# A two-layer hybrid encoder on one core: the opening's third transfer is made to wait for the first, and eighteen opening products stand for twenty-two

## The chip, the cores and the metric

The kernel runs on one core of a Trainium2 chip. The metric is the device time in microseconds (us). The kernel before was run three times; a run with the hardware profiler was taken beside these. The core has five engines that work side by side: TensorE (PE; its weight loads are listed as PEld), VectorE (DVE), ScalarE (ACT), GpSimd (POOL) and SyncE (SP). In this kernel SP computes nothing, it issues nearly all transfers from the chip's memory, one after another in a fixed order.

## The reference, cut to what matters

Two layers work on 256 frames of width 2048. In each, one wide input projection feeds three groups of heads, and one output projection joins them:

```python
h = x @ w_in
a_q, a_k, a_v, a_z, b_q, b_k, b_v, b_z, b_lr, m_q, m_z = jnp.split(h, cuts, axis=-1)
y_a = chunk_band_attention(heads_a(a_q), heads_a(a_k), heads_a(a_v), rel_table)
o_b = gla_chunk_recurrence(heads_k(b_q), heads_k(b_k), b_v, heads_k(log_g))
mkv = mem @ w_mem_kv
mk, mv = jnp.split(mkv, 2, axis=-1)
y_m = memory_attention(heads_m(m_q), heads_m(mk), heads_m(mv))
y = jnp.concatenate([y_a * silu(a_z), y_b * silu(b_z), y_m * silu(m_z)], axis=-1)
return layer_norm(DEEPNORM_ALPHA * x + y @ w_out, ln_g, ln_b)
```

The kernel does not begin with `x` but with `mem`, the 256 fixed memory tokens: the projection `mem @ w_mem_kv` is the first work of a layer. Its second half `mv` comes from the weights `G_MV`, its first half `mk` from `G_MK`. These activations and weights are what the opening transfers bring.

## The kernel before, in words

**Two-part products.** Every float32 matrix that TensorE multiplies is split into a high part, a rounded copy that ScalarE makes (a CAST), and a low part, the float32 rest that VectorE makes with one subtraction (a TENSOR_TENSOR). A product is then three TensorE products: high by high, low by high, high by low. So each transfer is followed by a cast, a subtraction and the products that read both.

**Tiles.** A weight load is 128 rows by 1024 float32 values, 512 KB, holding two steps of the contraction of 512 columns each. The memory tokens come transposed, 128 rows by 4 steps by 256 tokens, four such loads in all. In the names of the profile `raw` is a weight as it was transferred, `wh` and `wl` are its high and low parts, `res` is the space where activations land, and `x` holds their high and low parts. `memT` and `w` are the sources in the chip's memory.

**The ring.** `plan()` (L141) writes one list of loads in the order in which TensorE will use them: the first quarter of the memory tokens, the weights V0, V1, K0, the second quarter, V2, K1 and so on. `advance()` (L285) walks through the list with three marks: a load is cast three loads ahead of its use and subtracted two ahead, and its transfer is issued as soon as one of four `raw` buffers is free, that is when VectorE has made the low part of an earlier load. `start_load()` (L221) issues the transfer on SP at L238, `high()` (L248) casts at L261, `low()` (L263) subtracts at L268.

**The opening.** `begin()` (L339) replaces this for the first three loads. It cuts the first quarter of the memory tokens into its four steps, the tiles of the title, 128 KB each, and issues four transfers at L355 in this order: the first tile (128 KB), the first weights (512 KB), the other three tiles in one transfer (384 KB), and the second weights (512 KB). SP then goes on with the ring's third weights. While nothing has landed, TensorE runs `ZEROS` = 22 products of a constant by itself, 256 columns wide and in bfloat16, whose results are never read. After that, nine parts are cast (L362) and subtracted (L363): the first tile, the first half of the first weights' first step, its second half, their second step, the second tile, and so on to the second weights' second step. The first real products are 256 columns wide, twelve of them; after these come the first weights' second step with the second tile, and then the second weights with the third and the fourth tile, at 512 columns.

**Orders.** SP and TensorE execute their instructions in the order in which the program writes them. For VectorE, ScalarE and GpSimd a planner puts the instructions in order, with modelled times; the ring's casts and subtractions have priority there, and the subtractions of the ring keep the order among themselves. `later()` (L335) adds a dependency by hand: before the change it only makes GpSimd's first small transfers (gate weights and two vectors, L528 to L532) wait for the last cast of `begin()`.

Of the kernel before, what the change touches and what calls it, by code (L numbers as in the profile page):

```python
# [34 lines left out]
G_MK, G_MV, G_BQK, G_AQ0, G_AK0, G_AQ1, G_AK1, G_MQ, G_BZ, G_AZ0, G_AZ1, G_MZ, G_WO = range(13)  # L35
HI_AHEAD, LO_AHEAD, RAWS = 3, 2, 4
SUM_AHEAD, FIRST_SUM_AHEAD = 10, 20
ZEROS = 22
FILL = 5
AHEAD = 4000  # L40

# [11 lines left out]
def hybrid_trunk_kernel(  # L53
# [7 lines left out]
    pe, dve, act, pool, sp = nc.tensor, nc.vector, nc.scalar, nc.gpsimd, nc.sync  # L61
# [19 lines left out]
    def nm(s):  # L81
        uid[0] += 1
        return f"{s}_{uid[0]}"

    def mm(o, l, r, start, stop):
        pe.matmul(o, l, r, start=start, stop=stop, skip_group_check=True)  # L86
# [124 lines left out]
    def operand():  # L211
        return opp.tile([P, 4, 2, T], F32R, name=nm("x"), tag="x")
# [119 lines left out]

    begun = []

    def later(instruction):  # L335
        sync = mybir.DependencyInfo(mybir.DependencyClass.Sync, mybir.DependencyReason.DATA)
        tc.add_manual_dep(instruction.ins, begun[0].name, sync, reason="behind the first weights")

    def begin():  # L339

        x, ws = loads[0], loads[1:3]
        xt = operand()
        x.quarter[0].append(xt)
        x.hi, x.lo = xt[:, :, 0], xt[:, :, 1]
        x.raw = res.rearrange("p t (s j n) -> p (t s) j n", s=2, j=4)[:, 0]
        for w in ws:
            w.raw = wp.tile([P, 2, 512], F32, name=nm("raw"), tag="raw")
            w.hi = wp.tile([P, 2, 512], F32R, name=nm("wh"), tag="wh", bufs=4)
            w.lo = wp.tile([P, 2, 512], F32R, name=nm("wl"), tag="wl", bufs=3)
        one = nc.const_aps.tensor(1.0, [P, 256], mybir.dt.bfloat16)  # L350
        whole = slice(None)
        first, second = slice(0, 256), slice(256, 512)
        for d, s in ((x, (whole, 0)), (ws[0], (whole,)), (x, (whole, slice(1, 4))), (ws[1], (whole,))):
            src = d.src if d is x else d.src.rearrange("p (k n) -> p k n", k=2)
            sp.dma_start(d.raw[s], src[s])  # L355
        parts = [(x, (whole, 0)), (ws[0], (whole, 0, first)), (ws[0], (whole, 0, second)), (ws[0], (whole, 1)), (x, (whole, 1)),
                 (x, (whole, 2)), (ws[1], (whole, 0)), (x, (whole, 3)), (ws[1], (whole, 1))]
        at["dma"] = 3
        for i in range(ZEROS):
            mm(ps[:, 2 + i % 2, :256], one[:, :P], one, True, True)  # L360
        for d, s in parts:
            cast = act.copy(d.hi[s], d.raw[s])  # L362
            dve.tensor_tensor(d.lo[s], d.raw[s], d.hi[s].bitcast(F32), op=ALU.subtract)  # L363
        begun.append(cast.ins)
        at["hi"] = at["lo"] = 3
# [19 lines left out]
    def pair():  # L385
        side[0] = 2 - side[0]
        return side[0]
# [135 lines left out]
    def gla_inputs(l):  # L523
        gb = small([P, 2], "gb")
        ng = small([P, 1], "ng")
        raw = hd.tile([P, 256], F32, name=nm("gws"), tag="pairs0")
        for q in range(3):
            later(pool.dma_start(raw[32 * q:32 * q + 16], gate_w[l]))  # L528
            behind(act.copy(gw[32 * q:32 * q + 16], raw[32 * q:32 * q + 16]))
        behind(dve.tensor_tensor(gw[64:80], raw[64:80], gw[64:80].bitcast(F32), op=ALU.subtract))  # L530
        later(pool.dma_start(gb, gate_b[l]))
        later(pool.dma_start(ng, norm_g[l]))  # L532
        return gb, ng
# [443 lines left out]

    plan()
    begin()
    dve.memset(eps[:, 0:1], LN_EPS)  # L980
    dve.memset(eps[:, 1:2], RMS_EPS)
# [198 lines left out]
    d, c = side[0], pair()  # L1180
# [110 lines left out]
```

## Time and profile before

| what | value |
|---|---|
| median of three runs | 911.25 us |
| lowest and highest run | 911.09 and 912.42 us |
| the profiled execution's own time | 912.3 us |
| its span, first to last instruction | 910.4 us |
| TensorE busy | 903.4 us, 99% of the span |
| VectorE busy | 715.8 us, 79% |
| ScalarE busy | 549.6 us, 60% |
| read from memory | 193.16 MB, mean 214 GB/s over the span |

How to read it: a row of a timeline begins with the start and the duration in microseconds from the span's start, then the engine, the line of the kernel, the operation, what is written and what is read, the shape, and how many such instructions are merged. What stands in brackets is the idle time of that engine before the instruction, and what ended it. SPq rows are the issues of transfers; their duration is the issuing, not the transfer. A row of transfers gives size and microseconds from issue to landing. A row of windows gives a stretch, the busy time and number of instructions of each engine in it, the granted clock, the busy share of the sixteen transfer engines, and GB/s. A row of grouped instructions ends with the total busy time, the mean duration in nanoseconds, and the idle time before.

### The profile page before, as it was taken

The page shows a single profiled execution, that of the slowest core. Times are in us where ns is not written, and L with a number is a line of the kernel's source. Part 1 is how long each engine was busy: PE and PEld are TensorE (multiplying, and loading weights), DVE is VectorE, ACT ScalarE, POOL GpSimd, SP SyncE. Part 2 cuts the span into 40 slices and gives each one's busy share as a digit, 9 for nine tenths or more (in the row PEclk, how much of TensorE's full clock was granted, in tenths as well). Part 3 has the DMA queues.
Part 4 walks back from the last instruction along what each step waited for, and adds up shares of the span by engine and source line. Part 5 has one row for each costly group of instructions (what it writes and reads, how often), then busy time and mean ns, then how long its engine had stood idle before and what let it go on. Part 6 is the DMA issues. An engine that isn't in the chain of part 4 may idle for free.

```text
span 910.4 us, 14437 instructions
## 1 busy us (share of the span) xinstructions
PE 903.4 (99%) x5437; PEld 792.9 (87%) x5437; DVE 715.8 (79%) x990; ACT 549.6 (60%) x801; POOL 9.1 (1%) x24
## 2 busy tenths in 40 slices
PE   9999999999999999999999999999999999999997
PEld 7889999998888888888888899999988888888885
DVE  5697688798764877799978867886886769778996
ACT  5675655576575775655559655556756657665551
POOL 1000000000000000000000000000000000000000
PEclk9999999999999999999999999999999999999999
DMA  8868786775445457776765687666654565669752
GB/s 300 282 197 287 249 281 207 233 259 183 153 156 168 146 164 255 256 253 214 238 221 182 207 289 257 222 197 186 216 178 141 178 206 164 239 226 304 242 192 93
DMA packets 66853, 196.20 MB, mean 216 GB/s; under 512 B 7008, under 2 KB 9568, under 8 KB 66784
## 3 DMA queue, kind: packets, MB, share of 16 engines
q1 hardware_dynamic: 66400, 195.18, 65.3%
q8 instruction: 42, 0.69, 0.3%
q14 instruction: 27, 0.22, 0.1%
q0 software_dynamic: 384, 0.11, 0.1%
HBM read 193.16 MB, written 2.10 MB: 214 GB/s over the span
## 4 chain that ended last, share of the span: by engine, by line
PE 98%; DVE 1%; DMA 0%; ACT 0%; issue 0%; SPq 0%; ACTq 0%; DVEq 0%
PE ps L86 96%; PE ps L742 1%; DMA raw<-w 0%; PE ps L780 0%; PE ps L839 0%; DVE res L826 0%; DVE wl L268 0%; PE ps L711 0%; DVE x L268 0%; ACT res L886 0%; DVE sz L500 0%; PE ps L608 0%; PE ps L543 0%; ACT wh L362 0%; SPq L355 0%
## 5 line engine op out<-in xcount | busy, mean ns | idle before, releaser
L268 DVE TENSOR_TENSOR wl<-raw,wh 128x1024 fp32r<-128x1024 f32 (+1 forms) x313 | 365.0, 1169 | 120.3 <-PE ps L86 82.5
L261 ACT CAST wh<-raw 128x1024 fp32r<-128x1024 f32 (+1 forms) x313 | 314.0, 1008 | 229.1 <-PE ps L86 133.2
L86 PE MATMUL ps<-x,wh 128*128 128x512 f32 x1280 | 404.3, 397 | 0.0
L86 PEld LDWEIGHTS ps<-x,wl 128*128 128x128 f32 x1280 | 240.3, 188 | 57.0 <-DVE wl L268 0.5
L86 PE MATMUL ps<-wh,x 128*128 128x512 f32 (+2 forms) x984 | 287.1, 373 | 0.4 <-ACT wh L362 0.4
L86 PE MATMUL ps<-x,wl 128*128 128x256 f32 x1280 | 252.2, 278 | 0.1
L86 PEld LDWEIGHTS ps<-x,wh 128*128 128x128 f32 x1280 | 199.8, 189 | 1.6 <-issue 0.3
L86 PEld LDWEIGHTS ps<-wh,x 128*128 128x128 f32 x984 | 179.0, 188 | 24.2 <-ACT wh L362 0.8
L86 PE MATMUL ps<-wl,x 128*128 128x512 f32 (+2 forms) x492 | 182.8, 372 | 0.3 <-DVE wl L268 0.3
L86 PEld LDWEIGHTS ps<-wl,x 128*128 128x128 f32 x492 | 92.4, 188 | 13.5 <-DVE wl L268 0.7
L261 ACT CAST wh<-term 128x776 fp32r<-128x776 f32 (+1 forms) x39 | 36.0, 924 | 51.7 <-DVE term L260 43.3
L268 DVE TENSOR_TENSOR wl<-term,wh 128x776 fp32r<-128x776 f32 (+1 forms) x39 | 41.6, 1065 | 14.1 <-PE ps L86 13.6
L260 DVE TENSOR_TENSOR term<-term,term 128x776 f32<-128x776 f32 (+1 forms) x39 | 41.3, 1060 | 0.0
L86 PE MATMUL ps<-wh,s 128*128 128x512 f32 (+1 forms) x144 | 41.2, 367 | 0.0
L86 PEld LDWEIGHTS ps<-wh,s 128*128 128x128 f32 x144 | 25.8, 188 | 3.2
L86 PE MATMUL ps<-wl,s 128*128 128x512 f32 (+1 forms) x72 | 26.5, 368 | 0.0
L733 ACT ACTIVATE sc<-sc,mx 128x128 f32<-128x128 f32 (+1 forms) x32 | 14.2, 444 | 8.2 <-DVE mx L731 8.2
L86 PE MATMUL ps<-wh,sc 128*128 128x388 f32 x64 | 16.5, 338 | 0.0
L86 PEld LDWEIGHTS ps<-wl,s 128*128 128x128 f32 x72 | 13.5, 188 | 1.6
L500 DVE SCALAR_TENSOR_TENSOR sz<-ps,sz 128x512 f32<-128x512 f32 x20 | 13.7, 687 | 0.9
L86 PE MATMUL ps<-w,x 128*128 128x512 f32 (+1 forms) x72 | 14.3, 356 | 0.0
L858 DVE TENSOR_TENSOR res<-res,sc 128x512 f32<-128x512 f32 x16 | 10.4, 687 | 4.8 <-DMA sc<-ln_g 4.2
(224 smaller groups left out, 704.4 us busy)
## 6 DMA issues: line engine op xcount, KB each, us to landing
raw<-w SPq DMA_DIRECT2D x254, 512.0 KB, 4.3
raw<-w SPq DMA_DIRECT2D x64, 388.0 KB, 3.7
term<-w SPq DMA_DIRECT2D x24, 388.0 KB, 4.1
term<-w SPq DMA_DIRECT2D x15, 512.0 KB, 4.6
bias<-relw SPq DMA_DIRECT2D x16, 192.0 KB, 3.9
res<-xT SPq DMA_DIRECT2D x4, 512.0 KB, 7.0
res<-xn SPq DMA_DIRECT2D x4, 512.0 KB, 5.4
raw<-memT SPq DMA_DIRECT2D x4, 512.0 KB, 5.2
```

What stands on the lines that cost most here:

```text
L86: pe.matmul(o, l, r, start=start, stop=stop, skip_group_check=True)
L260: in_order(dve.tensor_tensor(d.raw, d.raw, d.plus, op=ALU.add))
L261: act.copy(d.hi, d.raw)
L268: in_order(dve.tensor_tensor(d.lo, d.raw, d.hi.bitcast(F32), op=ALU.subtract))
L500: dve.scalar_tensor_tensor(dst, a, scale, dst, op0=ALU.mult, op1=ALU.add)
L733: act.activation(s[:, own[t]], s[:, own[t]], AF.Exp, bias=mx[:, t:t + 1], accum_out=zs[:, t:t + 1])
L742: pe.transpose(ps[:, pt, i * P:(i + 1) * P], s[:, i * P:(i + 1) * P], ident)
L858: dve.tensor_tensor(r, r, row, op=op)
```

## The change

`later()` takes a second argument: the instruction to wait for, where it isn't the last cast of the opening. `begin()` keeps the four opening transfers in a list and makes the third one, the other three tiles, wait for the first one, the first tile. As SP issues in the written order, everything that SP issues after it comes after that wait as well. And `ZEROS` goes from 22 to 18.

```diff
-ZEROS = 22
+ZEROS = 18
...
-    def later(instruction):
+    def later(instruction, first=None):
         sync = mybir.DependencyInfo(mybir.DependencyClass.Sync, mybir.DependencyReason.DATA)
-        tc.add_manual_dep(instruction.ins, begun[0].name, sync, reason="behind the first weights")
+        tc.add_manual_dep(instruction.ins, (first or begun[0]).name, sync, reason="leaves the transfers to what is needed first")
...
+        opening = []
         for d, s in ((x, (whole, 0)), (ws[0], (whole,)), (x, (whole, slice(1, 4))), (ws[1], (whole,))):
             src = d.src if d is x else d.src.rearrange("p (k n) -> p k n", k=2)
-            sp.dma_start(d.raw[s], src[s])
+            opening.append(sp.dma_start(d.raw[s], src[s]))
+        later(opening[2], opening[0].ins)
```

## The prediction, made before the result was known

> **What bounds the kernel now.** I read the page's first and fourth parts first, then the chain that ended last in order of time, then the opening instruction by instruction.
>
> ```profile
> span 910.4 us, 14437 instructions
> PE 903.4 (99%) x5437; PEld 792.9 (87%) x5437; DVE 715.8 (79%) x990; ACT 549.6 (60%) x801; POOL 9.1 (1%) x24
> PE 98%; DVE 1%; DMA 0%; ACT 0%; issue 0%; SPq 0%; ACTq 0%; DVEq 0%
> ```
>
> TensorE is the bound. Only what moves its first useful product, or makes it wait later, can move the end. The chain begins like this:
>
> ```profile
> 0.74 0.39 SPq L355
> ...
> 1.18 4.25 DMA raw<-w
> ...
> 5.46 0.41 ACT wh L362
> 5.87 0.04 issue
> 5.92 50.58 PE ps L86 x262
> ```
>
> The first useful product starts at 5.92 and is set by the first weights: issued at 1.18, landed at 5.43, then the cast of its first 128x256 part. From there TensorE runs 50.58 us on end. So 0.49 us lies between the landing and the product.
>
> **The change part by part.** The changed edges sit in SP's opening issues, whose transfers took these times to land, in the same order (first tile, first weights, other three tiles, second weights):
>
> ```profile
> 0.74 0.39 SPq L355 DMA_DIRECT2D res<-memT  x1
> 1.18 0.42 SPq L355 DMA_DIRECT2D raw<-w  x1
> 1.65 0.42 SPq L355 DMA_DIRECT2D res<-memT  x1
> 2.12 0.43 SPq L355 DMA_DIRECT2D raw<-w  x1
> 2.59 0.43 SPq L238 DMA_DIRECT2D raw<-w  x1
> ```
>
> ```profile
> res<-memT SPq DMA_DIRECT2D x1, 128.0 KB, 2.2
> raw<-w SPq DMA_DIRECT2D x1, 512.0 KB, 4.3
> res<-memT SPq DMA_DIRECT2D x1, 384.0 KB, 5.4
> raw<-w SPq DMA_DIRECT2D x1, 512.0 KB, 6.2
> ```
>
> So they land at 2.94, 5.43 (by the chain), 7.05 and 8.3. For comparison, here is a 512 KB weight transfer that went out alone at 293.73, and a 388 KB one that went out alone in the window from 605.6:
>
> ```profile
> raw<-w SPq DMA_DIRECT2D x1, 512.0 KB, 3.5
> ...
> raw<-w SPq DMA_DIRECT2D x1, 388.0 KB, 3.1
> ```
>
> *The added wait.* SP issues in the order written, so the third issue now waits for 2.94 and goes out at about 3.0, 1.35 later. Behind it in SP's queue stand the second weights (to 3.46), and all later loads of the ring, each 1.35 later (the third weights from 2.59 to 3.93) until the ring's buffers hold SP anyway. Nothing else is issued by SP there.
>
> *The first weights.* Now they share the engines with what is issued 0.47 and 0.94 after them. What the engines moved:
>
> ```profile
> 1.00:2.00 1.00, 1.00 (x6) 0.68 (x5) 0.00 (x0) 1.00 (x1) 0.43 (x3) 1.00 0.14 24
> 2.00:3.00 1.00, 1.00 (x7) 0.72 (x5) 0.00 (x0) 0.04 (x2) 0.00 (x0) 1.00 0.87 243
> 3.00:4.00 1.00, 1.00 (x7) 0.67 (x6) 0.42 (x1) 0.38 (x1) 0.00 (x0) 1.00 0.71 287
> 4.00:5.00 1.00, 1.00 (x7) 0.67 (x5) 0.00 (x0) 0.00 (x0) 0.00 (x0) 1.00 1.05 390
> 5.00:6.00 1.00, 0.64 (x4) 0.23 (x2) 0.10 (x1) 0.54 (x2) 0.00 (x0) 1.00 0.91 335
> 6.00:8.00 2.00, 2.00 (x13) 1.57 (x13) 1.83 (x5) 1.61 (x5) 0.00 (x0) 1.00 1.02 342
> ```
>
> The last two columns are the engines' busy share and GB/s, which is kB per us. The first tile's 131 kB are reached at 2.0 + (131 - 24)/243 = 2.44 and landed at 2.94, 0.50 after. The first weights bring the sum to 655 kB, reached at 4.0 + (655 - 554)/390 = 4.26, yet they landed 1.17 after that, because part of what moved belonged to their successors. Alone, with the 0.50, they would land at 4.76. The lone row gives 1.18 + 3.5 = 4.68; the other bound is 5.43, nothing gained. I take 4.75, near both estimates: **0.68 us earlier**, and the first product could start at 4.75 + 0.49 = 5.24.
>
> *Four products fewer.* Opening products and their durations in two windows, the second of which holds the last ones; below them two real products of the same width, once the clock is open:
>
> ```profile
> 0.78 4.78 PE L86 MATMUL ps<-const-bfloat16-1.0 128*128 128x256 bf16 x22 [0.78 <-PEq L1281]
> ...
> 2.23 1.48 PE L86 MATMUL ps<-const-bfloat16-1.0 128*128 128x256 bf16 x6
> ```
>
> ```profile
> L86 PE MATMUL ps<-const-bfloat16-1.0 128*128 128x256 bf16 x4 | 1.1, 417 | 0.0
> ...
> L86 PE MATMUL ps<-const-bfloat16-1.0 128*128 128x256 bf16 x2 | 0.6, 380 | 0.0
> ```
>
> ```profile
> 7.30 0.40 PE L86 MATMUL ps<-wh,x 128*128 128x256 f32 x2
> 7.54 0.28 PE L86 MATMUL ps<-wl,x 128*128 128x256 f32 x1
> ```
>
> Six products in 1.48 with 0.417 for the last are one per 0.213. The twenty-second ends at 5.56, the eighteenth at 5.21 - 4 x 0.213 + 0.42 = 4.78. That is before 5.24, so the removal itself is worth nothing while the weights land later than 4.3. What it avoids is 5.56 - 5.24 = 0.32 us that twenty-two would have cost under the new landing. TensorE's idle gap becomes 0.46 us, after 0.36.
>
> *The other three tiles.* Their landing is bounded by 3.0 + 3.1 = 6.1 (the lone row of nearly the same size) and 3.0 + 5.4 = 8.4 (their own time now). The byte sum behind them, 1048 kB, is reached at 5.0 + (1048 - 944)/335 = 5.31; with a lag between 0.50 and 1.17 that is 5.8 to 6.5. I take 6.4. Now TensorE, ScalarE and VectorE show this:
>
> ```profile
> 8.00 0.19 PEld L86 LDWEIGHTS ps<-wh,x 128*128 128x128 f32 x1 [0.27 <-DVE x L363]
> ...
> 9.71 0.19 PEld L86 LDWEIGHTS ps<-wl,x 128*128 128x128 f32 x1 [0.23 <-DVE wl L363]
> ...
> 12.38 0.41 PEld L86 LDWEIGHTS ps<-x,wl 128*128 128x128 f32 x2
> ```
>
> ```profile
> 8.31 1.14 ACT L362 CAST wh<-raw 128x512 fp32r<-128x512 f32 x2 [0.21 <-DMA raw<-w]
> ...
> 10.74 1.23 DVE L268 TENSOR_TENSOR wl<-raw,wh 128x1024 fp32r<-128x1024 f32 x1 [0.48 <-ACT wh L261]
> ```
>
> Even now the weight load at 8.00 waits 0.27 for the second tile's low part. With a landing at 6.4 instead of 7.05 this point comes 0.65 earlier: it keeps nearly all of the 0.68.
>
> *The second weights.* This is the **term that decides**. The load at 9.71 waits 0.23 for their low part, which follows the landing at 8.3 through one cast and one subtraction. So TensorE is already level with this transfer, and an earlier start is kept only as far as this landing is earlier too. Bounds: 3.46 + 3.5 = 6.96 and 3.46 + 6.2 = 9.66. By bytes: 1573 kB are reached at 6.0 + (1573 - 1279)/342 = 6.86; now the lag is 1.45. The engines are full from 4.0 on, and by 4.26 they have moved as many bytes as the first two transfers hold, so the held-back ones find no hole: issued at 3.0, with the first tile's 1.0 to 1.3 from issue to first bytes (0.74, and 24 kB by 2.0), they start near 4.1. With a lag of 0.50 to 1.45 the landing is 7.4 to 8.3. I take 7.95, in the loaded half because the same loads stand behind it as now: **0.35 earlier**.
>
> *What comes after.* The third weights' low part is ready at 10.74 + 1.23 = 11.97 and loaded at 12.38, 0.4 to spare, which 0.35 uses up. Past that, the ring's loads go out when VectorE frees a buffer, and so move with TensorE.
>
> *The sum:* -0.35 us on the profiled execution's 912.3 us (span 910.4 and 1.9 around it), so 911.95. The runs' median is 911.25, below the profiled one; against it I forecast **910.9 us**. All bounds together: from -0.7 (everything follows the first product) to 9.66 - 8.3 = +1.35 (the second weights keep their 6.2 us), 910.55 to 912.6.
>
> **Rivals.** A. *The whole 0.68 is kept:* the second weights land by 7.6. For it: the lag of 0.50 without load. Against: the same three loads are queued behind them. 910.55.
>
> B. *Nothing is kept:* the wait isn't in SP's stream, or the first weights are slow for a reason of their own (engines only 0.71 busy from 3.0 to 4.0, with two transfers outstanding, speaks for that), or a later VectorE limit swallows it. That limit is here:
>
> ```profile
> 59.82 0.30 PEld L86 LDWEIGHTS ps<-x,wl 128*128 128x128 f32 x2 [0.52 <-DVE wl L268]
> ...
> 50.00:55.00 5.00, 5.00 (x6) 1.00 0.49 136
> ...
> 51.08 1.22 DVE L504 TENSOR_TENSOR mv<-ps,mv 128x1024 fp32r<-128x1024 f32 x1
> ```
>
> VectorE has no gap from 50 to 55 and TensorE waits for it at 59.82. 911.25.
>
> C. *Slower, by the transfers:* the second weights land late. It decides from 8.3 on; at 9.66 TensorE waits 1.35 at what is now 9.71, at 8.8 0.5. For it: the first transfers of the program took 2.2, 4.3, 5.4, 6.2, and a stream started anew at 3.0 might ramp again. 911.75 to 912.6.
>
> D. *Slower, by the planner's order:* ScalarE's and VectorE's orders are planned from modelled times, which this change moves. One mv subtraction of 1.22 put ahead of the weights' one in VectorE's full stretch costs TensorE 1.2 at 59.82, less the 0.35. 912.1; two such swaps pass 0.2%.
>
> E. *The clock.* Now the last products shorten to a mean of 380 ns, so the clock opens near 5.4, 4.6 us after the first product. Eighteen end at 4.78 with the clock shut. If the idle 0.46 starts the count anew, it opens at 5.24 + 4.6 = 9.8: the first twelve products at 0.213 end at 7.8, six of double width at 0.427 are not done at 9.8 but at 10.1, and twelve more at 0.23 end at 12.9 where now 12.14: +0.76, 912.0. Against it: at 5.4 TensorE has been busy for all but 0.46 of its last 4.6 us.
>
> [...]
>
> **How the numbers follow.** Forecast 0.48, A 0.14, B 0.16, C 0.08, D 0.08, E 0.06. The predicted time is the forecast's. The range goes from A less 0.35 for the spread of runs (911.09 to 912.42) to the far ends of C and D: 910.2 to 912.4. A measurement of this kernel can tell about 0.2%, 1.8 us, from no change; none of the forecast, A, B, C and E reaches that. Only a changed order (D) in several places would: slower 0.07, faster 0.04 where it happens to spare stalls; within 0.2% 0.89.
>
> **What would show it.** SP's third issue near 3.0 with its predecessor's landing as releaser; the first weights landing near 4.75 and the first product near 5.24; the opening products ending at 4.78; a weight load near 9.4 that still waits for the second weights' low part; products of 256 at 0.12 spacing from 5.5 on. Wrong if the first weights still land after 5.2, if the second land after 8.3, if the first products are spaced 0.213, or if the wait at 59.82 has changed by more than what TensorE gained.

## The result and the profile after

The changed kernel takes **913.41 us** (median of 12 runs, 912.01 to 915.51), the kernel before 911.25 beside it (12 runs, 910.97 to 912.42): a ratio of **1.0023**, 95% interval 1.0015 to 1.0031. It is slower by 2.16 us, a little more than the 0.2% that can be told from no change. The forecast was 910.9 with a range up to 912.4. The profiled execution took 913.7 against 912.3, with spans of 911.8 and 910.4. In what follows, one execution of the changed kernel at 1825.8 us and two of the kernel before at 1505.5 and 1505.8 were slow throughout; they are counted in the medians but in no ratio, mean or share below.

The page's first and fourth parts for the kernel after:

```profile
span 911.8 us, 14429 instructions
PE 903.6 (99%) x5433; PEld 792.4 (87%) x5433; DVE 715.5 (78%) x990; ACT 550.0 (60%) x801; POOL 9.1 (1%) x24
PE 98%; DMA 1%; DVE 1%; ACT 0%; issue 0%; ACTq 0%; DVEq 0%
```

At this height nothing has changed: TensorE is still the bound and is busy for as long. Its chain of waits, though, begins otherwise:

```profile
0.74 2.28 DMA res<-memT
3.04 4.98 DMA res<-memT
8.50 49.02 PE ps L86 x250
...
60.88 112.44 PE ps L86 x642
```

Before, the chain came from the first weights to a product at 5.92. Now it comes from the first tile's landing to the held-back three tiles, which take 4.98 us to land, and the piece of TensorE's work that runs on begins only at 8.50. (The chain counts TensorE as running on through a short wait at 10.76, for the second weights' low part, shown below; it is the last wait of the opening.) The stretch that began at 59.82 - a wait stood there before - now begins at 60.88, 1.06 later, and the chains stay 1.05 apart up to about 330. So this part of the loss is made in the opening. The spans differ by 1.4; the other 0.35 come later and are within what two executions differ by there (see the rule below the table). The opening in order of time (start, duration, what; in brackets the idle time and its releaser):

```profile
0.78 4.00 PE L86 MATMUL ps<-const-bfloat16-1.0 128*128 128x256 bf16 x18 [0.78 <-PEq L1283]
...
3.04 0.33 SPq L356 DMA_DIRECT2D res<-memT  x1
3.41 0.43 SPq L356 DMA_DIRECT2D raw<-w  x1
...
4.83 1.23 ACT L364 CAST wh<-raw 128x256 fp32r<-128x256 f32 x3 [1.38 <-DMA raw<-w]
...
5.29 0.51 PE L86 MATMUL ps<-wh,x 128*128 128x256 f32 x2 [0.51 <-ACT wh L364]
...
6.67 0.40 PE L86 MATMUL ps<-wh,x 128*128 128x256 f32 x2
...
6.91 0.28 PE L86 MATMUL ps<-wl,x 128*128 128x256 f32 x1
8.04 1.02 ACT L364 CAST x<-res 128x256 fp32r<-128x256 f32 x3 [1.98 <-DMA res<-memT]
...
8.50 0.19 PEld L86 LDWEIGHTS ps<-wh,x 128*128 128x128 f32 x1 [1.51 <-ACT x L364]
...
9.36 1.14 ACT L364 CAST wh<-raw 128x512 fp32r<-128x512 f32 x2 [0.30 <-DMA raw<-w]
...
10.76 0.19 PEld L86 LDWEIGHTS ps<-wl,x 128*128 128x128 f32 x1 [0.34 <-DVE wl L365]
...
13.17 0.62 PE L86 MATMUL ps<-x,wh 128*128 128x512 f32 x2
```

The first product comes 0.63 earlier, as forecast. Then the three tiles (cast at 8.04, before at 7.09) and the second weights (cast at 9.36, before at 8.31) come later, and TensorE idles: 1.31 us before the products at 8.50 (its weight load, shown, 1.51). The last row is the first product with the third weights, where the opening ends and the ring takes over. In the kernel before it stands 1.03 earlier:

```profile
12.14 0.62 PE L86 MATMUL ps<-x,wh 128*128 128x512 f32 x2
```

Where the transfers lost this is in the windows (the last two columns are the transfer engines' busy share and GB/s):

```profile
1.00:2.00 1.00, 1.00 (x6) 0.68 (x5) 0.00 (x0) 1.00 (x1) 0.44 (x3) 1.00 0.13 36
2.00:3.00 1.00, 1.00 (x7) 0.72 (x5) 0.00 (x0) 0.02 (x1) 0.00 (x0) 1.00 0.82 190
3.00:4.00 1.00, 1.00 (x7) 0.67 (x6) 0.42 (x1) 0.41 (x1) 0.00 (x0) 1.00 0.93 365
4.00:5.00 1.00, 0.78 (x4) 0.23 (x2) 0.00 (x0) 0.17 (x1) 0.00 (x0) 1.00 0.59 173
5.00:6.00 1.00, 0.71 (x4) 0.55 (x5) 0.73 (x2) 1.00 (x3) 0.00 (x0) 1.00 0.94 277
6.00:8.00 2.00, 1.19 (x10) 0.98 (x9) 0.72 (x2) 0.06 (x1) 0.00 (x0) 1.00 1.02 339
8.00:10.00 2.00, 1.50 (x6) 1.05 (x6) 1.09 (x3) 1.66 (x5) 0.00 (x0) 1.00 1.03 373
```

From 4 to 5 the engines move 173 kB where they moved 390 before, and their share falls from 1.05 to 0.59: the first two transfers are through, and the held-back ones, issued at 3.04 and 3.41, move little yet. The last window of the kernel before reads:

```profile
8.00:10.00 2.00, 2.00 (x9) 1.52 (x9) 1.65 (x4) 1.59 (x4) 0.24 (x1) 1.00 1.05 414
```

By 10.0 the kernel after has moved 36 + 190 + 365 + 173 + 277 + 2 x 339 + 2 x 373 = 2465 kB, the kernel before 24 + 243 + 287 + 390 + 335 + 2 x 342 + 2 x 414 = 2791. The 326 kB missing are 0.8 to 0.9 us at the 373 and 414 of the last windows.

### The profile page after: what moved, and what is told of

It is laid out like the page before. It is cut to its first block, busy times and chain, and to the rows that moved or that the text cites. A ratio compares the mean times of both kernels' runs of the same rounds, so it can differ in the third digit from the quotient of the medians.

```text
span 911.8 us, 14429 instructions
## 1 busy us (share of the span) xinstructions
PE 903.6 (99%) x5433; PEld 792.4 (87%) x5433; DVE 715.5 (78%) x990; ACT 550.0 (60%) x801; POOL 9.1 (1%) x24
## 4 chain that ended last, share of the span: by engine, by line
PE 98%; DMA 1%; DVE 1%; ACT 0%; issue 0%; ACTq 0%; DVEq 0%
PE ps L86 96%; DMA res<-memT 1%; PE ps L744 1%; PE ps L782 0%; PE ps L841 0%; DVE res L828 0%; DVE wl L268 0%; PE ps L713 0%; DVE sz L502 0%; DVE x L268 0%; PE ps L610 0%; ACT res L888 0%; PE ps L545 0%; ACT x L364 0%; ACTq L1289 0%
## 5 line engine op out<-in xcount | busy, mean ns | idle before, releaser
L502 DVE SCALAR_TENSOR_TENSOR sz<-ps,sz 128x512 f32<-128x512 f32 x20 | 13.6, 686 | 0.9
L582 ACT ACTIVATE sc<-sc 128x512 f32<-128x512 f32 x12 | 7.6, 631 | 10.9 <-DVE sc L580 10.9
```

Of the source, the lines that this page charges most:

```text
L502: dve.scalar_tensor_tensor(dst, a, scale, dst, op0=ALU.mult, op1=ALU.add)
L582: act.activation(dd, dd, AF.Abs)
```

## The experiments

All edits are against the changed kernel. Each median stands against the kernel before, run beside it (12 to 35 runs of it). The table has, from each profiled execution: the issue of the three tiles, the first real product, the start of the second weights' cast, and the first product with the third weights. (In w11 the second weights come in two halves, and both casts are given.)

| run | median, less before | tiles issued | first product | second weights cast | third weights' product |
|---|---|---|---|---|---|
| before | | 1.65 | 5.92 | 8.31 | 12.14 |
| before, again (b2) | -0.56 | 1.65 | 5.73 | 7.65 | 11.61 |
| 26 products, no wait (w10) | +0.02 | 1.65 | 5.85 | 8.07 | 11.87 |
| 18, no wait (w2, w2b) | +0.40, +1.12 | 1.65, 1.64 | 5.76, 5.80 | 8.10, 8.28 | 11.90, 13.23 |
| 22 and the wait (w1, w1b) | +0.89, +1.35 | 2.90, 3.00 | 5.44, 5.16 | 9.09, 8.91 | 12.91, 12.72 |
| 30 and the wait (w8, w8b) | +0.51, +1.59 | 2.88, 2.94 | 6.06, 5.97 | 8.89, 9.37 | 12.70, 13.16 |
| the change | +2.16 | 3.04 | 5.29 | 9.36 | 13.17 |
| the change, again (a2, a3, a4) | +1.75, +1.49, +2.00 | 3.02, 2.94, 2.90 | 5.30, 5.22, 5.40 | 8.95, 9.31, 10.22 | 12.75, 13.12, 15.38 |
| short hold, 22 (w4) | +0.77 | 2.25 | 5.19 | 8.68 | 12.48 |
| long hold, 22 (w5) | +2.02 | 4.89 | 5.35 | 9.71 | 14.97 |
| fourth held, 18 (w3) | +1.24 | 1.65 | 5.64 | 9.32 | 13.15 |
| order of use, 18 (w7) | +1.39 | in parts | 4.43 | 8.20 | 12.01 |
| second queue, 22 (w9) | +0.43 | 0.75 | 6.39 | 7.22 | 12.29 |
| two queues, halves, 20 (w11) | +0.32 | 0.75 | 5.75 | 7.40, 8.30 | 11.64 |

**One rule fits the table.** The last column is the later of two: the first product + 5.9 (TensorE's own work without a stop: w9, w11, b2), and the second weights' cast + 3.8 (all others, within 0.03). Three executions lie 1.1 to 1.5 above it, and these are explained below. What follows that product, the span less the last column, takes 897.4 to 899.0 in these profiles, without a pattern by kernel (before and b2 898.3 and 898.4, the change's four 897.8 to 898.6). So the kernels differ by what is made before it; but the rest moves by up to 1.6 us from execution to execution, so a single span does not order them.

### Each part alone

The wait alone, with twenty-two products (w1, w1b), and the products alone (w2, w2b):

```diff
-ZEROS = 18
+ZEROS = 22
```

```diff
-        later(opening[2], opening[0].ins)
```

> The wait as in the change, but twenty-two opening products. Theory 1 (the held-back transfers land late, TensorE is tied to them): the product count is idle; the other three tiles land near 8.0 and the second weights near 9.3 as in the changed kernel, TensorE restarts near 8.5, median 913.4 (+2.2 on the kernel before), within 0.4 of the changed kernel. Theory 2 (too few opening products, clock or idle gap): back to 911.3.

> The wait with twenty-two products once more, beside the changed kernel. By late transfers alone: the same median as the changed kernel in this call, within 0.4. By too few opening products: 0.8 to 1.2 below it.

> Eighteen opening products, no wait. Theory 1: the transfers land as before (first weights 5.43, three tiles 7.05, second weights 8.3), first product 5.92, median 911.3, within 0.4 of the kernel before. Theory 2: TensorE idles 1.1 us before its first product, the first real products are spaced 0.213 instead of 0.12, and the median is 912.5 to 913.5.

> Eighteen products without the wait once more. If four products fewer cost nothing: the median of the kernel before in this call, within 0.3. If they cost by themselves: 0.4 to 1.2 above it.

The wait alone gives 1.0013 (1.0004 to 1.0022) and 1.0011 (1.0002 to 1.0020), the products alone 1.0005 (0.9996 to 1.0014) and 1.0011 (1.0002 to 1.0020). The wait alone, its window and its opening:

```profile
4.00:5.00 1.00, 0.70 (x7) 0.38 (x4) 0.00 (x0) 0.01 (x1) 0.00 (x0) 1.00 0.80 131
```

```profile
9.09 1.14 ACT L364 CAST wh<-raw 128x512 fp32r<-128x512 f32 x2 [0.39 <-DMA raw<-w]
...
12.91 0.61 PE L86 MATMUL ps<-x,wh 128*128 128x512 f32 x2
```

The same hole from 4 to 5 (131 kB), the same late second weights: this part belongs to the wait. In the eight profiles with the change's wait this window moves 130 to 179 kB, in the five without a hold and in the old order 324 to 390 (w2: 349). The engines are not simply idle in it: their busy share is 0.54 to 0.89. The landings came about as expected for late transfers (tiles cast at 7.67, second weights at 9.09), but w1's median did not: 912.42, where 913.0 to 913.8 was expected.

The first profile of eighteen products alone had an opening like before's. The second had its loads in time (8.28, before 8.31) and yet ended at 13.23:

```profile
0.78 3.46 PE L86 MATMUL ps<-const-bfloat16-1.0 128*128 128x256 bf16 x18 [0.78 <-PEq L1282]
...
5.80 0.50 PE L86 MATMUL ps<-wh,x 128*128 128x256 f32 x2 [1.57 <-ACT wh L363]
...
8.28 1.14 ACT L363 CAST wh<-raw 128x512 fp32r<-128x512 f32 x2 [0.77 <-DMA raw<-w]
```

```profile
3.60:6.90 3.30, 1.73 (x13) 1.25 (x12) 1.47 (x4) 1.65 (x6) 0.00 (x0) 1.00 1.03 363
7.00:10.20 3.20, 3.20 (x12) 2.72 (x12) 2.59 (x6) 2.22 (x5) 0.48 (x1) 0.50 1.03 384
10.40:13.60 3.20, 3.20 (x15) 2.62 (x15) 2.79 (x3) 2.37 (x3) 1.99 (x4) 1.00 1.02 391
```

The clock opened early here. The granted clock (the column ahead of the transfers' share) does not show an opening: it reads 1.00 in every window from 1.0 to 6.0 of all nineteen profiles, also while opening products still follow each other at 0.21 us. Their pace shows it: the window from 3 to 4 holds nine of them here and seven in the kernel after, and the eighteen ran out at 4.24 instead of 4.78. TensorE then idled 1.57, was busy for 1.73 of 3.30, and from 7.0 to 10.2 the granted clock was at 0.50. By the rule this opening would have ended at 12.1; the **shut clock** cost 1.1.

With means of 0.73 from 6 to 8 and 0.91 from 10 to 12, the stretch at 0.50 goes from 6.9 to 10.4, about 3.4 us. In it four real products of 256 columns take 0.86, from 7.17 to 8.03: they are spaced 0.21, like the first opening products, where those of the kernel after are spaced 0.12. That is why a change of pace from 0.21 to 0.12 is called an opening of the clock here. The stretch ahead of the one at 0.50 was not idle throughout, and what shut the clock was not shown.

Twenty-six products without the wait:

```diff
-ZEROS = 18
+ZEROS = 26
...
-        later(opening[2], opening[0].ins)
```

> No wait, twenty-six products. If idle stretches before the first product cost by shutting the clock in some runs: no worse than the kernel before, 911.2 to 911.7, with fewer runs above 912.3. If every product past the landing of the first weights delays TensorE: they end at 5.6 to 6.4, up to 0.5 after the first weights' cast, 911.7 to 912.2.

It measured 1.0004 (0.9995 to 1.0012), the kernel before within 0.02. Runs above 912.3 were not fewer (3 of 11, before 3 of 32). More products than twenty-two win nothing that shows.

### The size of the hold

The products were built ahead of the transfers, and the third transfer waited for the sixth of them (w4), or it waited for the first weights (w5), both with twenty-two products; or only the fourth transfer waited for the first tile (w3):

```diff
-        later(opening[2], opening[0].ins)
+        later(opening[2], idle[5].ins)
```

```diff
-        later(opening[2], opening[0].ins)
+        later(opening[2], opening[1].ins)
```

```diff
-        later(opening[2], opening[0].ins)
+        later(opening[3], opening[0].ins)
```

> The third transfer waits for the sixth opening product (ends at 2.2) instead of the first tile's landing (2.94): issue near 2.3, 0.65 later than before, 0.75 earlier than in the changed kernel; twenty-two products. Theory 1, as a hole in the transfers that opens only when the first weights are through before the next bytes come (about 1.3 after issue): first bytes at 3.6, before the first weights end at 4.3, no hole, second weights at 8.0 to 8.5, median 911.0 to 911.6. If the loss is a plain delay, one for one with the issue: second weights at 8.8, median 912.3.

> The third transfer waits for the first weights' landing instead of the first tile's: issue near 4.85 instead of 3.04, twenty-two products. Theory 1: now the whole added delay of 1.8 is an empty stretch of the transfers; three tiles land near 9.8, second weights near 11.1, TensorE restarts near 10.3, median 915.2 (913.4 + 1.8). If the loss of the changed kernel isn't from late transfers: no more than 914.

> The wait is moved from the third transfer to the fourth: the other three tiles go out at 1.65 as before, the second weights at 3.0, eighteen products. If what is late is whatever stands behind the wait: three tiles near 6.5, TensorE passes the second tile without the long idle stretch, but the second weights land at 8.8 to 9.3 and TensorE waits there for 0.8 us; median 912.2 to 912.7. If only the held-back tiles matter: second weights by 8.3, median 911.5.

Ratios: short 1.0009 (1.0000 to 1.0018), long 1.0020 (1.0010 to 1.0029), the fourth alone 1.0010 (1.0002 to 1.0019). Without a hold the second weights are cast at 8.08 in the mean of five profiles. A hold of 0.6 puts that at 8.68, the change's hold of about 1.3 at 9.26 (mean of eight), one of 3.2 at 9.71: nearly one for one at first, half for the long one.

The short hold decides between the two ideas of its expectation. That of a hole which opens only when the held-back bytes come too late for the engines had 8.0 to 8.5 and at most 911.6; the plain delay had 8.8 and 912.3. Measured are 8.68 and 912.30, and the window from 4 to 5 moves only 172 kB even with the issue at 2.25. The plain delay held. The long hold, issue, windows and landing:

```profile
4.89 0.33 SPq L356 DMA_DIRECT2D res<-memT  x1
...
9.71 1.14 ACT L364 CAST wh<-raw 128x512 fp32r<-128x512 f32 x2 [0.24 <-DMA raw<-w]
```

```profile
5.00:6.00 1.00, 0.65 (x3) 0.48 (x4) 0.67 (x2) 1.00 (x3) 0.00 (x0) 1.00 0.08 25
...
10.40:13.60 3.20, 3.20 (x9) 2.42 (x9) 2.49 (x3) 2.51 (x3) 2.44 (x5) 0.50 1.03 408
```

```profile
res<-memT SPq DMA_DIRECT2D x1, 384.0 KB, 3.5
```

The engines stood idle (0.08) and then took 3.5 us for the 384 KB. In the kernel after, the same transfer:

```profile
res<-memT SPq DMA_DIRECT2D x1, 384.0 KB, 5.0
```

So the stream that starts anew beside the end of the first weights was slower than the one on idle engines (4.2 to 6.0 in the eight profiles with the change's wait, 3.5 in w5). Why was not settled. The long hold's expected landing (11.1) and time (915.2) fell with this: the second weights took 4.4 us instead of 5.9 and were cast at 9.71. Its other branch, no more than 914 if late transfers were not the cause, has the measured 913.55, but the late cast is in the profile. That profile also has the clock shut, at 0.50 from 10.4 to 13.6, 1.45 above the rule, with twenty-two products.

Holding the fourth alone costs as much as the wait: the tiles came in time (cast at 6.33), the second weights at 9.32. That transfer is the one that counts. Here is its window from 4 to 5 and its time to land:

```profile
4.00:5.00 1.00, 0.78 (x4) 0.23 (x2) 0.00 (x0) 0.00 (x0) 0.00 (x0) 1.00 1.02 406
```

```profile
raw<-w SPq DMA_DIRECT2D x1, 512.0 KB, 6.2
```

In the kernel after, the same transfer:

```profile
raw<-w SPq DMA_DIRECT2D x1, 512.0 KB, 5.9
```

So with the tiles not held there is no hole from 4 to 5, and the second weights are as late all the same. What stays alike is their own time from issue to landing: 5.5 to 6.2 in the five profiles without a hold, 5.5 to 6.9 in the eight with the change's wait, 5.9 in the mean of both. They land later by about as much as they are issued later. The missing bytes go with the wait, but they are not needed for the delay; whether the loads issued right behind take a share of the engines from this one was not isolated.

### More products under the wait, and the change again

```diff
-ZEROS = 18
+ZEROS = 30
```

> The changed kernel with thirty opening products, which end at 7.3 instead of 4.8, so that TensorE has almost no idle stretch before the second tile comes. If late transfers alone set the time: the products cover a wait, the second weights' low part is waited for at 10.3 all the same, median 912.7 to 913.4 as the other kernels with the wait. If part of the loss comes from TensorE's idle stretches (clock): 0.5 or more below the changed kernel in the profile's marks and 912.3 or less as median.

> The wait with thirty products once more. If TensorE's idle stretches make part of the loss: again 0.6 to 1.2 below the changed kernel's 913.4, that is 912.2 to 912.8, and 0.5 to 0.9 above the kernel before, which is then the price of the late transfers alone. If the 912.2 was chance: 913.0 to 913.4.

> The changed kernel once more, beside the other runs of this call, and a second look at its opening. If the wait alone cost 0.9 and four products fewer another 1.2, this gives 913.0 to 913.7 again; if the two kernels with the wait differ only by the chance of their runs, this gives about 912.5, as the wait alone did. In the trace: other three tiles issued near 3.0, landing 7.5 to 8.1; second weights 8.8 to 9.4.

> The changed kernel, third look. One of its runs in four took over 914.4. If such a run is one whose clock shut or opened late in the opening: a look with an early opening of the clock (before 3.8) shows a shut clock near 7 to 10 and over 914. If it is one whose transfers landed later still: three tiles after 8.3, clock open throughout.

> The changed kernel, fourth look, same question: late landing (three tiles after 8.3) or a shut clock. A look of 913.0 to 913.7 should show three tiles 7.5 to 8.1, second weights 8.9 to 9.3, clock open.

Thirty products: 1.0013 (1.0004 to 1.0022) and 1.0012 (1.0003 to 1.0021). The first product was held up to 6.06, 0.90 later than in w1b, with the second weights at the same moment (8.89 and 8.91), and the opening ended alike (12.70 and 12.72): under the wait, an **earlier first product is worth nothing**. Of the two expectations, the first median fell on the side of the clock (912.22), the second on that of chance (913.1), so whether thirty products spare the shut clock is not told.

The change again: 1.0018 (1.0009 to 1.0027), 1.0016 (1.0006 to 1.0026) and 1.0020 (1.0009 to 1.0031). The third profile (a3, 912.84 us) was neither of the two kinds asked for; the last (a4) fell on an execution of 915.69 us, near the top of the change's runs. Its opening and its windows:

```profile
0.78 3.41 PE L86 MATMUL ps<-const-bfloat16-1.0 128*128 128x256 bf16 x18 [0.78 <-PEq L1283]
...
8.90 1.02 ACT L364 CAST x<-res 128x256 fp32r<-128x256 f32 x3 [2.73 <-DMA res<-memT]
...
9.36 0.19 PEld L86 LDWEIGHTS ps<-wh,x 128*128 128x128 f32 x1 [2.25 <-ACT x L364]
...
15.38 0.62 PE L86 MATMUL ps<-x,wh 128*128 128x512 f32 x2
```

```profile
7.00:10.20 3.20, 1.16 (x6) 0.64 (x5) 0.86 (x3) 1.02 (x3) 0.00 (x0) 1.00 1.01 357
10.40:13.60 3.20, 3.20 (x9) 2.43 (x8) 2.31 (x4) 2.78 (x4) 1.94 (x4) 0.50 0.99 347
```

Here both met. The eighteen products ran out at 4.19, the tiles landed later than in any other profile, TensorE was busy for 1.16 of 3.20, and then the clock was shut, at 0.50 from 10.4 to 13.6: 1.35 above the rule on top of second weights that were late by themselves.

### Where the opening's limit lies

The opening transfers in halves, in the order of use, with no wait (w7); the three tiles on ScalarE's queue (w9, with twenty-two products and no wait); and both ideas together, with the tiles' casts kept behind those of the first weights (w11, twenty products, no wait). And the kernel before once more (b2).

```diff
-        for d, s in ((x, (whole, 0)), (ws[0], (whole,)), (x, (whole, slice(1, 4))), (ws[1], (whole,))):
+        for d, s in ((x, (whole, 0)), (ws[0], (whole, 0)), (x, (whole, 1)), (ws[0], (whole, 1)), (x, (whole, slice(2, 4))),
+                     (ws[1], (whole, 0)), (ws[1], (whole, 1))):
```

```diff
-            opening.append(sp.dma_start(d.raw[s], src[s]))
+            opening.append((act if len(opening) == 2 else sp).dma_start(d.raw[s], src[s]))
```

```diff
+        for d, s in ((x, (whole, 0)), (x, (whole, slice(1, 4))), (ws[0], (whole, 0)), (ws[0], (whole, 1)), (ws[1], (whole, 0)), (ws[1], (whole, 1))):
...
+            opening.append((act if len(opening) == 1 else sp).dma_start(d.raw[s], src[s]))
...
             cast = act.copy(d.hi[s], d.raw[s])
+            casts.append(cast)
+            if d is x and len(casts) > 3:
+                later(cast, casts[2].ins)
```

> No wait; instead the opening goes out in the order of use and in smaller pieces: first tile, first weights' first step (256 KB), second tile, first weights' second step, third and fourth tile, second weights' two steps; eighteen products. If order, not a wait, is what brings the first weights earlier: first step lands near 4.0 to 4.3, first product near 4.8, second weights' first step by 7.8; 0.2 to 0.5 below the kernel before, 910.8 to 911.1. If smaller rows or three more issues cost as much as they bring: 911.3 to 912.0.

> The opposite of the change: no wait, and the other three tiles are issued by ScalarE's own queue at about 0.75 instead of SP's third place at 1.65, so that SP issues the second weights at 1.65 and the third at 2.12; twenty-two products. By the slope of the runs so far (each us of later issue puts the third weights 0.4 to 0.6 later): third weights cast near 9.4, median 0.2 to 0.4 below the kernel before, 911.2. If the first weights are slowed by the tiles beside them as much as the later loads gain: first product at 6.2, median 911.5 to 912.

> The kernel before, for a second look at its opening: how far the landings move from one execution to the next. Three tiles 6.5 to 7.1, second weights 8.0 to 8.4, third weights cast near 9.5, and the median of the call.

> Nothing waits; the three tiles are issued by ScalarE's queue at about 0.75 beside SyncE's, the first and second weights come in halves of 256 KB, twenty opening products, and the casts of the three tiles are kept behind those of the first weights, so that ScalarE's order is that of the kernel before. Theory: the loads set the opening's end. With the second queue the third weights were cast at 8.54 where the kernel before has 9.0 to 9.7; there the first product, held to 6.39 by ScalarE's order, was the bound, and the step to the next weights took 5.9 from it. Here the first product should come near 5.2 (768 KB moved by 4.3, 0.5 to land, 0.4 to cast), and the first product of the next weights at 11.0 to 11.3, 0.6 to 0.9 before the kernel before: a median 0.6 to 0.9 us below it, less than can be told with certainty. Rival: the moment of the loads is shared, not won; halves and a second queue bring the third weights back to 9.5 or later, and the median lies at the kernel before's or up to 1 us above, as with the transfers in the order of use on one queue.

Ratios: order of use 1.0013 (1.0004 to 1.0022), second queue 1.0009 (1.0000 to 1.0018), before again 0.9997 (0.9987 to 1.0007), two queues 1.0003 (0.9994 to 1.0012). None beats the kernel before. The order of use:

```profile
4.43 0.71 PE L86 MATMUL ps<-wh,x 128*128 128x256 f32 x2
...
8.87 0.30 PEld L86 LDWEIGHTS ps<-wh,x 128*128 128x128 f32 x2 [1.48 <-ACT wh L364]
```

The first product comes 1.5 earlier than before, and all of it gone by the second weights: the third weights' product stands at 12.01, between the two profiles of the kernel before. Right behind it TensorE waits for the third weights' low part, 0.65 us that the kernel before does not have there:

```profile
12.85 0.30 PEld L86 LDWEIGHTS ps<-x,wl 128*128 128x128 f32 x2 [0.65 <-DVE wl L268]
```

Both branches of its expectation, 912.0 at most, were missed. (This profile is of its fastest execution, 911.63; it need not show all that the median, +1.39, lost.) In w9 the second weights were cast early (7.22), but ScalarE cast all tiles first, and the first product at 6.39 set the end. The kernel with two queues was to have both early:

```profile
4.36 0.40 ACT L364 CAST x<-res 128x256 fp32r<-128x256 f32 x1 [1.91 <-DMA res<-memT]
...
5.75 0.50 PE L86 MATMUL ps<-wh,x 128*128 128x256 f32 x2 [1.33 <-ACT wh L364]
...
9.65 1.05 ACT L261 CAST wh<-raw 128x1024 fp32r<-128x1024 f32 x1 [0.72 <-DMA raw<-w]
```

That expectation fell: the first tile, cast near 3 with one queue, was cast at 4.36. Beside the tiles' transfer, issued at the same moment, it took 3.6 us to its cast instead of 2.2; in w9 the tiles' casts began at 4.64, 3.9 after the issue. The first product came at 5.75 instead of 5.2, the third weights at 9.65 instead of 8.5. Its rival held. In these runs, what one transfer won another lost.

## Why the prediction was wrong

**What held.** The third issue (forecast 3.0, measured 3.04), the first weights' landing (4.75; their cast began at 4.83), the first product (5.24; 5.29), the opening products' end (4.78; 0.78 + 4.00), the third weights' low part that is still in time, and no changed order: VectorE, ScalarE, GpSimd and SP execute the same sequence of operations, tiles and shapes in both traces, which excludes rival D. The opening products' end is partly luck: in two other profiles of the same kernel it is 4.65 and 4.19. The wait at 59.82 moved with TensorE, by 1.06, so B's later limit played no part, nor did its slow first weights. A fell with the step that follows.

**The step that failed** is the term called decisive, *the second weights*: forecast 7.95, bounds 6.96 to 9.66, measured 9.33 (cast at 9.36). That it decides was right: the opening ends 3.8 after this cast, before (8.31 to 12.14) and after (9.36 to 13.17). Its size was wrong by 1.4 us, and its reason with it. The forecast let the transfer take 4.5 us from its issue (7.95 - 3.46) instead of 6.2; it took 5.9. That it keeps its time stood in the sum only as the outer bound. In the sum's own terms, 1573 kB are reached at 7.57 (1041 by 6.0, then 339 per us) instead of 6.86, 0.7 late, and the lag behind that is 1.76, outside the 0.50 to 1.45 allowed; the forecast used 1.09.

The reason, "the held-back ones find no hole", took the engines as full from 4.0 on, from windows in which those very transfers did the filling. Take them away and the window from 4 to 5 moves 173 kB, not 390. That is only half of the miss: with the fourth alone held (w3) the bytes are reached at 6.96, nearly as forecast, and the lag is 2.3. The three tiles went the same way: 6.4 forecast, 8.02 measured (3.04 + 4.98), near their upper bound of 8.4, which was their own time under load. The sum named a new hole's time (issue at 3.0, first bytes near 4.1) but put no price on it.

**C was the mechanism**, slower by the transfers, with its place and price: landing at 9.66 costs 1.35, at 8.8 0.5; by that line 9.33 costs 1.03, and 1.03 is what the profile shows. Its reason, that a stream started anew may be slow again, is supported by the windows with the wait, but w3 is as late without the hole, so how much of the delay it makes stays open. It was given 0.08: the last rows before the change (full engines) were weighed above the first ones (the slow start of the streams, 24 and 243 kB in the windows from 1 to 3).

**What C leaves.** The medians lost more, 2.16, 1.75, 1.49 and 2.00, a mean of 1.85. The four runs with the wait and more products lost 0.51 to 1.59, a mean of 1.09, which is C: the end of the opening with the clock open is 12.93 in the mean of seven profiles with the wait, 11.88 in the mean of four without, 1.05 apart. The rest, about 0.76, is as much as eighteen products lost without the wait (0.40 and 1.12). That the eighteen add to the wait is not resolved by any one comparison. Taken over all executions it is: each less the mean of the kernel before beside it, the change's 38 lie 1.80 above, the 44 with the wait and more products 1.11, a difference of 0.69 with a 95% interval of 0.26 to 1.12. Eight of the 38 lie above 914.4, one of the 44, none of the 22 with eighteen products and no wait. Two of the eight profiles with eighteen products show one way: the clock opens early, they run out early (at 4.24 in w2b, 4.19 in a4), TensorE idles (1.57 and 1.21 before the first real product, 2.04 more in a4), and later the clock reads 0.50 for over 3 us (7.0 to 10.2 in w2b, 10.4 to 13.6 in a4), at 1.1 to 1.4 each. How often that happens, whether the early end brings it about, and whether it is the whole 0.7, stays open: in w2 the eighteen ran out at 4.36 without it, and the long hold with twenty-two shows that it is not theirs alone.

**E** was near this, but not as put. In the profile after, the clock is open during the first real products: from 6.67 to 6.91 two products of 256 columns take 0.24, so the idle 0.51 before them did not start 4.6 us anew. A late opening is seen once: in a3 the real products follow each other at 0.21 up to 6.7 (three take 0.64 from 6.06). It cost nothing there, as TensorE then waited for the tiles until 8.46, and the opening ended by the rule (9.31 to 13.12). Lost time stood beside the reverse, an early opening (w2b and a4, 1.1 and 1.4). The step *four products fewer* costed the removal at nothing with the clock opening at 5.4; an earlier opening was not weighed.

**The range** was said to end at the far ends of C and D, but stopped at 912.4, while C's own far end was 912.6. It added nothing for the spread of runs on that side. The change's spread is wider (3.5 us, before 1.5), and both effects can meet.

## What to carry to other kernels

Holding transfers back brought the first weights' cast from 5.46 to 4.83 here, and the second weights, issued 1.29 later, were cast 1.05 later. Price a held-back transfer first with its own time from issue to landing as it is now (here 5.9 in the mean, without a hold and with the change's wait), and take windows in which it has a part as no proof that the engines stay full without it (here 390 kB became 173). Find which load sets the end of an opening before making another one early: here the second weights did, and a first product up to 1.5 us earlier bought nothing. The eighteen opening products ended at anything from 4.19 to 4.78 in the eight profiles that have them: size such work for the execution where it runs out early, too.

## What was not expected of the hardware

- The clock opened at quite different moments in executions of one kernel. Eighteen opening products ended at 4.78 in the kernel after and at 4.19 in the same kernel's last profile, and in its third (a3) products were still spaced 0.21 up to 6.7. It also read 0.50 after stretches in which TensorE was busy for 1.16 of 3.20 (a4), 1.56 of 3.20 (w5) or 1.73 of 3.30 (w2b), not idle throughout.
- The 384 KB took 3.5 us on idle engines (w5), and 5.0 in the kernel after and 5.98 in the change's last profile when issued at about 3.0. The long hold's 3.5 comes nearest to the 3.1 of the 388 KB that went out alone before, and none of those issued at about 3.0 (4.2 to 6.0) comes near it.
- Landings of the same program moved: the second weights of the kernel before were cast at 8.31 and at 7.65.
- Busy transfer engines moved very different amounts: with the wait (w1) they were 0.80 busy from 4 to 5 and moved 131 kB, in w3 1.02 busy and moved 406.
